# Forty weight sums moved from the first output projection to the gate and up pass

## The chip, the cores and the metric

The kernel runs on one core of a Trainium2 chip. The metric is device time in microseconds for one execution; the time of a kernel is the median of its runs. TensorE (PE in the profile) does the matrix products, VectorE (DVE) and ScalarE (ACT) work on tiles and read PE's accumulators out of PSUM, GpSimd (POOL) and SyncE (SP) mainly start DMAs. ACT can start DMAs too. Every engine executes its own list of instructions in order.

## The reference

Two layers of a backbone over 1024 latent tokens and 256 context tokens, model width 1024. Layer 0 mixes by Fourier groups and a long convolution, layer 1 by neighbourhood attention. Each mixer ends in an output projection with a gated residual, and each layer in a SwiGLU feed-forward block of width 2816:

```
h = h + g1 * (mixer(modulate(rms_norm(h))) @ w_out)
u = modulate(rms_norm(h))
h = h + g2 * ((silu(u @ w_gate) * (u @ w_up)) @ w_down)
```

In layer 0 context tokens run through the same weights as latent ones. The final RMSNorm of the latent stream is the output.

## The kernel before

Activations lie with the model dimension on partitions. Products that need float32 accuracy are made of half-precision pairs: an operand x is scaled by s, rounded to a 16-bit high part, and the rest is the low part; three products replace one. `half_split` makes a pair, the high part on ACT (line 1227) and the low part on DVE (line 1228). For s, the kernel bounds each weight block by sums of absolute values over its rows. `abs_sums` takes such a sum on ACT (line 1260, Abs with an accumulator column); a few columns are later added up over the partitions by a small matmul and inverted (`over_partitions`, `scale_cols`, `qkv_scales`, `first_scales`).

The stages around the change, in program order:

- The input projection of layer 0, with `gate_sums` woven in: the first 32 sums of layer 0's gate and up blocks, loaded by DMAs that ACT starts (`lda`, line 271) into two tiles, summed in place (line 1297).
- Convolution and Fourier stages.
- The first output projection, `out_proj`: two groups of token columns, first context and the first 512 latent tokens, then the second 512. Each group loops over eight weight blocks of 512 KB. A block is loaded by SP (`ld`), cast on ACT (line 287) with the remainder on DVE (line 289), and multiplied on PE (line 283); the accumulators are added to the residual on DVE (line 1206), squared on ACT for the coming norm (line 505) and added up (line 510). Once in each of the sixteen blocks, `next(fill, None)` advances a filler.
- That filler is `qkv_sums`: 12 sums that are left of layer 0's gate and up blocks, then 40 sums of 128x1024 tiles that layer 1 needs: 8 tiles each of the value, query, key and second output weights, and 8 of layer 1's first gate and up blocks. Each tile comes by a POOL DMA (`ldr`, line 274) into one of the 20 large tiles (`S4`). With the filler's step, the first group covers the 12 and 16 of the 40, the second group the other 24.
- The feed-forward block of layer 0, `ffn(0, ...)`. It first makes context's pass (a loop over 22 column blocks, gate and up weights split by `weights3`, with the second half of the latent operand preparation, `wino_second`, between them), and then the gate and up pass of the latent tokens: 11 rounds `i`, each with one gate and one up block of 256 columns multiplied by a seven-product scheme (`wino_steps`, line 1482; PSUM is copied by ACT at line 1487). In every round weights are fetched one step ahead, `finish` closes the round before, `sums` takes four sums of the down weights and the round's values are summed too.
- In the last round `qkv_scales` reads the sums of the 40 tiles that belong to the attention; `first_scales(1)` reads the eight of layer 1's gate and up blocks after the pass.

The order of instructions on each engine is fixed when the program is built. The program's order gives the priorities; a planner that estimates the time of every instruction places them by these and by readiness, and gives each tile a free buffer of its pool. `follow` ties instructions behind another where the program wants that. Small tiles (`S2`, 128x512 float32) have a pool of 34 buffers; `T` gives tiles from a smaller pool; `C` reserves columns for good, and `pad` fills up that area to a fixed width.

Of the kernel before, what the change touches and what calls it, by code (L numbers as in the profile page):

```python
# [14 lines left out]
AF = mybir.ActivationFunctionType  # L15
# [9 lines left out]
NFB = 22  # L25
# [4 lines left out]
WID = {0: 512, 1: 512, 2: 256, 3: 256, 4: 256}  # L30
OFF = {0: 0, 1: 512, 3: 512, 4: 768}
KSTART = (0, 8, 24, 32)
PAD_C, PAD_T, SHIFT = 136, 160, 16
BOPS = ("B11", "B21", "T2", "T1", "T3", "B22", "T4")


# [165 lines left out]
class Builder:  # L202
# [1059 lines left out]
    def qkv_sums(self):  # L1262

        a = self.a
        self.qs = self.C(40)
        src = [a["wv"][ch, kp] for ch in range(2) for kp in range(4)]
        src += [a[n][b] for n in ("wq", "wk", "w_out2") for b in range(KB)]
        src += [a[n][1, 2 * i + k] for i in (0, 1) for n in ("gate", "up") for k in (0, 1)]
        todo = [(a[("gate", "up")[j // 2 % 2]][0, j // 4 * 2 + j % 2], self.fs[:, j:j + 1])
                for j in range(32, 4 * (NFB // 2))]  # L1270
        todo += [(x, self.qs[:, k:k + 1]) for k, x in enumerate(src)]
        for j, (x, col) in enumerate(todo):
            t = self.S4()
            self.ldr(t, x)
            self.abs_sums([t], col)
            if j % 4 == 3 if j < 16 else j % 3 == 0:
                yield
        yield

    def gate_sums(self):  # L1280

        nc, a = self.nc, self.a
        n = 32
        self.fs = self.C(4 * (NFB // 2))
        tiles = {}

        def load(j):
            if j < n:
                t = tiles[j] = self.pw.tile([P, 1024], F32, tag="ws", name=self.nm("ws"))
                self.lda(t, a[("gate", "up")[j // 2 % 2]][0, j // 4 * 2 + j % 2])  # L1290

        load(0)
        load(1)
        yield
        for j in range(n):
            t = tiles.pop(j)
            nc.scalar.activation(t, t, AF.Abs, scale=2.0 ** -15, accum_out=self.fs[:, j:j + 1])
            load(j + 2)
            if j % 2:
                yield  # L1300

    def first_scales(self, l):

        keys = [(l, i, m) for i in range(2 if l else NFB // 2) for m in (0, 1)]
        n, k = len(keys), 3 * len(self.wsc)
        q = self.qs[:, 32:40] if l else self.fs
        s, inv = self.scale_cols(q, self.wcol, k, n)
        for j, key in enumerate(keys):
            self.wsc[key] = (s[:, j:j + 1], inv[:, j:j + 1])

    def qkv_scales(self):

        nc = self.nc
        bounds = self.over_partitions(self.qs[:, :32].rearrange("p (i k) -> p i k", k=1))
        t = self.C(8)
        nc.vector.tensor_reduce(t[:, :4], bounds.rearrange("p (i k) -> p i k", k=8), axis=AX, op=MAX)
        nc.vector.tensor_scalar(t[:, :4], t[:, :4], 1e-30, None, op0=MAX)
        nc.vector.reciprocal(t[:, 4:8], t[:, :4])
        self.u1col, usi = self.operand_scale(1, 0, (0, 1))
        c = self.C(3)  # L1320
        nc.vector.tensor_scalar(c[:, 2:3], t[:, 1:2], usi, 0.125, op0=MUL, op1=MUL)
        nc.vector.tensor_scalar(c[:, 0:1], c[:, 2:3], t[:, 2:3], usi, op0=MUL, op1=MUL)
        nc.vector.tensor_scalar(c[:, 1:2], t[:, 0:1], t[:, 3:4], usi, op0=MUL, op1=MUL)
        self.wscale = {n: t[:, 4 + j:5 + j] for j, n in enumerate(("wv", "wq", "wk", "w_out2"))}
        self.qinv, self.oinv = c[:, 0:1], c[:, 1:2]
# [198 lines left out]
    def ffn(self, l, u, h, hs, second, after, keep=None, begun={}):  # L1524

        nc, a = self.nc, self.a
# [6 lines left out]
        def sums(i):  # L1533

            w = a["down"][l]
            t = [self.S2() for _ in range(4)]
            a21, a22, a11, a12 = t
            with self.follow(self.last_ld):
                for x, (k, r) in zip(t, ((0, 1), (1, 1), (0, 0), (1, 0))):
                    self.ld(x, w[2 * i + k, r])  # L1540
            if i < nh:
                self.abs_sums(t, sums_of[:, 4 * i:4 * i + 4])
            nc.vector.tensor_tensor(a22, a21, a22, ADD)  # L1543
            nc.vector.tensor_tensor(a21, a11, a21, SUB)
            nc.vector.tensor_tensor(a11, a22, a11, SUB)
            nc.vector.tensor_tensor(a12, a12, a11, SUB)
            for k, x in (("S1", a22), ("S2", a11), ("S3", a21), ("S4", a12)):
                self.ldr(sops[i][k], x)

        todo = iter(())  # L1550
        if l == 0:
            self.pad(self.pt, PAD_T)
        if u is not None:
            for fb in range(NFB):
# [6 lines left out]
                t = self.T()  # L1561
# [8 lines left out]
            todo = (x for m in range(6) for x in self.ada_group(1, m, (0, 1) if m < 2 else (0,), "s4"))  # L1570

        def finish(i, gate):

            up = self.res
            inv = self.wsc[(l, i, 1)][1]
            for k, g in gate.items():
                nc.vector.scalar_tensor_tensor(g, up[k], inv, g, op0=MUL, op1=MUL)
            if i < nh:
                self.abs_sums(list(gate.values()), sums_of[:, 4 * (nh + i):4 * (nh + i) + 4])
            b11, b12, b21, b22 = gate[(0, 1)], gate[(0, 0)], gate[(1, 1)], gate[(1, 0)]  # L1580
            t1, t2, t4 = up[(0, 0)], up[(0, 1)], up[(1, 1)]
            nc.vector.tensor_tensor(t1, b12, b11, SUB)
            nc.vector.tensor_tensor(t2, b22, t1, SUB)
            nc.vector.tensor_tensor(t4, b21, t2, SUB)
            nc.vector.tensor_tensor(b12, b22, b12, SUB)
            for k, t in zip(BOPS, (b11, b21, t2, t1, b12, b22, t4)):
                self.ldr(bops[i][k], t)

        prev = None
        waiting = {}  # L1590

        def fetch(i, m):
            b = begun.get((i, m))
            if i < n2 and (b is None or not b.whole):
                g = self.weights_ahead((l, i, m), b.w) if b else self.wino_weights((l, i, m))
                next(g)
                waiting[(i, m)] = g

        fetch(0, 0)
        for i in range(n2):  # L1600
            g, up = begun.get((i, 0)), begun.get((i, 1))
            if g is None or not g.whole:
                wg = waiting.pop((i, 0))
                w = next(wg)
                next(wg)
            fetch(i, 1)
            if g is None:
                g = Steps(self.wino_steps(w, self.G))
                g.to(1)
            if prev is not None:  # L1610
                prev[0].to(7)
                finish(i - 1, prev[1])
            wu = waiting.pop((i, 1))
            w = next(wu)
            if up is None:
                up = Steps(self.wino_steps(w, self.TK))
            if i == 0:
                for k, _ in enumerate(second):
                    if k == 11:
                        next(wu)  # L1620
            next(wu, None)
            fetch(i + 1, 0)
            for k in (3, 4, 5) if i == 0 and l == 1 else ():
                g.to(k)
                up.to(k)
            g.to(5)
            up.to(1)
            if i == n2 - 1:
                scales = self.down_scales(l, nh)
                if l == 0:  # L1630
                    self.qkv_scales()
            g.to(7)
            gate = dict(self.res)
            inv = self.wsc[(l, i, 0)][1]
            for k in ((0, 0), (1, 1), (0, 1)):
                nc.scalar.activation(gate[k], gate[k], AF.Silu, scale=inv)
            t = self.G()
            nc.scalar.activation(t, gate[(1, 0)], AF.Silu, scale=inv)
            gate[(1, 0)] = t
            up.to(5)  # L1640
            prev = (up, gate)
            for k in (2 * i - 2, 2 * i - 1) if l == 1 else (9, 10) if i == 9 else (i,) if i < 9 else ():
                if 0 <= k < n2:
                    sums(k)
            for _ in range(2):
                next(todo, None)
# [903 lines left out]
```

## Time and profile before

| | us |
|---|---|
| median of 3 runs | 2923.67 |
| lowest and highest run | 2923.64, 2932.0 |
| profiled execution | 2921.78 |
| its span in the trace | 2920.0 |
| first output projection on PE | about 738 to 870 |
| context's pass on PE | about 875 to 998 |
| latent gate and up pass on PE, layer 0 | about 998 to 1389 |

The profile gives, for a stretch of the span, the busy time of each engine, the clock that PE was granted (1.00 is full speed), and the share of time in which the sixteen DMA engines were busy. A timeline row is start, duration, engine, line, operation, output and input tile; a bracket at its end gives the engine's idle time before it and what ended that.

### The profile page before, as it was taken

How to read it: one execution, taken by the hardware profiler on the slowest of the kernel's cores; microseconds unless marked ns; L12 is line 12 of the kernel's file. 1: busy time of each engine (PE TensorE's matmuls, PEld its weight loads, DVE VectorE, ACT ScalarE, POOL GpSimd, SP SyncE). 2: the span in 40 equal slices, each digit the busy share in tenths (PEclk: the TensorE clock that was granted, in tenths of full speed). 3: DMA queues.
4: the chain of work that ended last, by engine and by line, in shares of the span. 5: the costliest groups of instructions: out<-in, count | busy, mean ns of one | idle time of the engine just before them, and what ended most of it. 6: DMA issues, size and time to landing. Idle time of an engine off the chain costs nothing. (4 is left out here: it accounts for less than half of the span.)

```text
span 2920.0 us, 45967 instructions
## 1 busy us (share of the span) xinstructions
PE 2762.0 (95%) x16143; PEld 1692.6 (58%) x16143; DVE 2092.4 (72%) x3753; ACT 1653.6 (57%) x2899; POOL 644.9 (22%) x1065
## 2 busy tenths in 40 slices
PE   6979999999989999999999999999999999999998
PEld 3755546888868744444555844676665444444554
DVE  5767848586357798886886767777777688775755
ACT  4674544454666655554555554777664477654543
POOL 1011103254320121122120012454442022112000
PEclk8989999999989999999999999999999999999999
DMA  7585655357886665556995798777775666425753
GB/s 264 184 285 192 242 173 164 116 173 247 329 320 226 207 223 195 208 210 235 324 340 186 254 345 307 172 187 177 188 198 183 230 244 234 146 94 182 239 188 116
DMA packets 330915, 636.95 MB, mean 218 GB/s; under 512 B 91574, under 2 KB 131192, under 8 KB 330682
## 3 DMA queue, kind: packets, MB, share of 16 engines
q1 hardware_dynamic: 252378, 384.38, 40.6%
q0 software_dynamic: 71392, 228.65, 22.0%
q10 hardware_dynamic: 6912, 20.97, 2.1%
q8 instruction: 127, 2.08, 0.3%
q14 instruction: 106, 0.87, 0.1%
HBM read 476.30 MB, written 135.53 MB: 210 GB/s over the span
## 5 line engine op out<-in xcount | busy, mean ns | idle before, releaser
L1482 PE MATMUL ps<-s,s 128*128 128x512 f16 x2064 | 464.2, 379 | 5.3 <-ACT g L1487 3.2
L1482 PEld LDWEIGHTS <-s 128*128 128x128 f16 x2640 | 257.9, 98 | 319.1 <-issue 7.3
L283 PE MATMUL ps<-s,wh 128*128 128x256 f16 (+3 forms) x1752 | 396.4, 331 | 15.8 <-ACT wh L1227 9.9
L283 PEld LDWEIGHTS <-wh 128*128 128x128 f16 x2368 | 231.2, 99 | 194.1 <-ACT wh L1227 27.8
L1227 ACT ACTIVATE s<-s,c 128x512 f16<-128x512 f32 (+1 forms) x324 | 234.5, 752 | 137.8 <-DMA s<-d 75.3
L1699 PE MATMUL ps<-s 128*128 128x512 f16 (+2 forms) x1308 | 303.4, 378 | 2.0 <-DVE s L1228 2.0
L1228 DVE SCALAR_TENSOR_TENSOR s<-s,c,s 128x512 f16<-128x512 f32 (+1 forms) x324 | 247.4, 794 | 78.0 <-ACT s L1227 77.1
L283 PE MATMUL pq<-s,wh 128*128 128x512 f16 (+1 forms) x1000 | 281.2, 355 | 8.9 <-ACT t L1913 3.8
L283 PE MATMUL ps<-s,wl 128*128 128x256 f16 (+3 forms) x876 | 261.0, 331 | 0.5 <-DVE wl L289 0.5
L1699 PEld LDWEIGHTS <-s 128*128 128x128 f16 x1536 | 148.4, 98 | 179.0 <-issue 7.0
L274 POOL DMA_DIRECT2D d<-s x201 | 108.6, 541 | 619.2 <-DVE s L1543 200.2
L283 PE MATMUL ps<-s,s 128*128 128x65 f16 (+5 forms) x2666 | 223.0, 236 | 23.0 <-ACT s L287 5.9
L1482 PE MATMUL ps<-s,wh 128*128 128x512 f16 x616 | 186.6, 381 | 4.2 <-ACT wh L1227 4.2
L335 ACT CAST mat<-cs 128x1024 fp32r<-128x1024 f16 (+2 forms) x120 | 111.5, 935 | 134.3 <-PE ps L283 49.0
L283 PE MATMUL ps<-s,mat 128*128 128x512 f32 x696 | 181.3, 406 | 6.0 <-DVE s L289 5.4
L283 PE MATMUL pq<-s,wl 128*128 128x512 f16 (+1 forms) x500 | 174.8, 355 | 0.0
L283 PEld LDWEIGHTS <-wl 128*128 128x128 f16 x1184 | 117.6, 99 | 82.2 <-issue 6.0
L283 PEld LDWEIGHTS <-s 128*128 128x128 f16 x2400 | 114.2, 98 | 77.3 <-issue 9.7
L283 PEld LDWEIGHTS ps<-s,mat 128*128 128x128 f32 x696 | 133.9, 195 | 40.6 <-DVE s L289 6.8
L1260 ACT ACTIVATE t<-s 128x1024 bf16<-128x1024 f32 (+1 forms) x152 | 129.0, 849 | 38.3 <-DMA s<-in_down 19.6
L283 PEld LDWEIGHTS ps<-s,s 128*128 128x128 f32 (+1 forms) x746 | 114.6, 194 | 33.8 <-ACT s L287 7.1
L1482 PE MATMUL pq<-s,s 128*128 128x512 f16 x576 | 132.8, 380 | 0.3 <-ACT s L1227 0.2
(433 smaller groups left out, 5471.6 us busy)
## 6 DMA issues: line engine op xcount, KB each, us to landing
s<-d SPq DMA_DIRECT2D x294, 256.0 KB, 4.2
d<-s POOLq DMA_DIRECT2D x157, 256.0 KB, 3.8
s<-in_down SPq DMA_DIRECT2D x154, 256.0 KB, 4.9
s<-in_ada_w POOLq DMA_DIRECT2D x48, 512.0 KB, 4.9
g<-in_bias POOLq DMA_DIRECT2D x128, 192.0 KB, 3.5
s<-in_gate SPq DMA_DIRECT2D x46, 512.0 KB, 3.8
s<-in_up SPq DMA_DIRECT2D x46, 512.0 KB, 5.4
d<-g POOLq DMA_DIRECT2D x87, 256.0 KB, 2.7
```

The costliest lines, as they stand in the source:

```text
L274: self.last_ldr = self.nc.gpsimd.dma_start(out, in_).ins
L283: self.nc.tensor.matmul(o, l, r, start=st, stop=sp)
L335: self.nc.scalar.copy(m, st)
L1227: nc.scalar.activation(hi, src, AF.Copy, scale=scale)
L1228: self.last_lo = nc.vector.scalar_tensor_tensor(lo, src, scale, hi, op0=MUL, op1=SUB).ins
L1260: self.nc.scalar.activation(junk[:, :t.shape[1]], t, AF.Abs, scale=2.0 ** -15, accum_out=st[:, k:k + 1])
L1482: nc.tensor.matmul(ps, x[:, sl], y, start=first and j == 0 and x is wh and y is xh, stop=j == 3 and x is wl, skip_group_check=True)
L1699: m = nc.tensor.matmul(acc[j][:, c0:c1], x[:, sl], y[:, xs], start=first and k == 0, stop=last and k == 2, skip_group_check=True)
```

## The change

The 40 sums leave the filler of the output projection and become a filler of the gate and up pass of layer 0.

- `qkv_sums` keeps the 12 sums, two for each of the first six blocks.
- A new generator `later_sums` cuts each of the 40 tiles into two halves of 128x512. Four `S2` tiles form a ring for all 80 halves. A half is loaded by a DMA on ACT's queue (`lda`), summed in place on ACT into a column of its own, and the half four places on is loaded into the same tile.
- `ffn` of layer 0 creates the generator behind context's pass; its first step starts four loads. `some()` takes two halves at each of four places of a round, so that the 80 are used up in the first ten rounds; before `qkv_scales` whatever is left would be taken.
- There are 80 sum columns instead of 40, and the scales add two columns for each tile. `PAD_C` is smaller by 40 columns, so that the area keeps its width.

The name of the change also speaks of context's pass in half-precision pairs. That pass is already computed so in the kernel before (`weights3`), and the diff does not touch it.

```diff
-PAD_C, PAD_T, SHIFT = 136, 160, 16
+PAD_C, PAD_T, SHIFT = 96, 160, 16
...
     def qkv_sums(self):
         a = self.a
-        self.qs = self.C(40)
+        for j in range(32, 4 * (NFB // 2)):
+            t = self.S4()
+            self.ldr(t, a[("gate", "up")[j // 2 % 2]][0, j // 4 * 2 + j % 2])
+            self.abs_sums([t], self.fs[:, j:j + 1])
+            if j % 2:
+                yield
+        yield
+
+    def later_sums(self):
+        a, nc = self.a, self.nc
+        self.qs = self.C(80)
         src = [a["wv"][ch, kp] for ch in range(2) for kp in range(4)]
         src += [a[n][b] for n in ("wq", "wk", "w_out2") for b in range(KB)]
         src += [a[n][1, 2 * i + k] for i in (0, 1) for n in ("gate", "up") for k in (0, 1)]
-        todo = [(a[("gate", "up")[j // 2 % 2]][0, j // 4 * 2 + j % 2], self.fs[:, j:j + 1])
-                for j in range(32, 4 * (NFB // 2))]
-        todo += [(x, self.qs[:, k:k + 1]) for k, x in enumerate(src)]
-        for j, (x, col) in enumerate(todo):
-            t = self.S4()
-            self.ldr(t, x)
-            self.abs_sums([t], col)
-            if j % 4 == 3 if j < 16 else j % 3 == 0:
-                yield
+        src = [x[:, c:c + 512] for x in src for c in (0, 512)]
+        ring = [self.S2() for _ in range(4)]
+        for t, x in zip(ring, src):
+            self.lda(t, x)
         yield
+        for j in range(len(src)):
+            t = ring[j % 4]
+            nc.scalar.activation(t, t, AF.Abs, scale=2.0 ** -15, accum_out=self.qs[:, j:j + 1])
+            if j + 4 < len(src):
+                self.lda(t, src[j + 4])
+            yield
...
-        q = self.qs[:, 32:40] if l else self.fs
+        q = self.qs[:, 64:80] if l else self.fs
...
-        bounds = self.over_partitions(self.qs[:, :32].rearrange("p (i k) -> p i k", k=1))
+        bounds = self.over_partitions(self.qs[:, :64].rearrange("p (i k) -> p i k", k=2))
...
+        later = self.later_sums() if l == 0 else iter(())
+        next(later, None)
+
+        def some(n=2):
+            for _ in range(n):
+                next(later, None)
...
             fetch(i, 1)
+            some()
...
             fetch(i + 1, 0)
+            some()
...
             g.to(5)
             up.to(1)
+            some()
             if i == n2 - 1:
+                some(80)
                 scales = self.down_scales(l, nh)
...
             prev = (up, gate)
+            some()
```

## The prediction

> **What bounds the kernel now.** I read the page, then stretches of ten microseconds around the first output projection, the waits and timelines there, and last the stretches of the gate and up pass, which receives the work.
>
> ```profile
> span 2920.0 us, 45967 instructions
> PE 2762.0 (95%) x16143; PEld 1692.6 (58%) x16143; DVE 2092.4 (72%) x3753; ACT 1653.6 (57%) x2899; POOL 644.9 (22%) x1065
> ```
>
> TensorE (PE) is busy for 95% of the span, so a change that leaves the matmuls alone gains only where PE stands still or runs slowly. The next rows are: stretch, its length, busy time of PE, PEld, DVE, ACT and POOL (with instructions), PE's granted clock, share of the DMA engines, GB/s.
>
> ```profile
> 740.00:800.00 60.00, 60.00 (x344) 52.37 (x343) 22.70 (x34) 42.99 (x78) 17.13 (x32) 1.00 0.84 335
> 812.00:874.00 62.00, 52.19 (x201) 40.16 (x198) 35.64 (x57) 44.84 (x80) 17.04 (x32) 0.91 0.80 318
> ...
> 830.00:840.00 10.00, 8.00 (x29) 6.03 (x28) 7.40 (x10) 7.53 (x14) 5.01 (x10) 0.83 1.01 402
> 860.00:870.00 10.00, 7.60 (x24) 5.53 (x24) 1.76 (x3) 7.04 (x13) 1.63 (x3) 0.83 1.03 420
> 870.00:880.00 10.00, 6.72 (x32) 5.28 (x33) 4.13 (x5) 6.41 (x11) 0.55 (x1) 0.66 1.03 419
> 880.00:890.00 10.00, 8.06 (x52) 5.55 (x51) 5.50 (x7) 7.46 (x12) 0.54 (x1) 0.84 1.01 408
> 920.00:930.00 10.00, 10.00 (x94) 8.96 (x92) 9.12 (x12) 6.07 (x9) 1.08 (x2) 1.00 0.55 185
> ```
>
> The projection's first group (context and the first 512 tokens, 740 to 800) has busy DMA engines and ACT at 43 of 60 us, and PE does not notice: 60 of 60 at clock 1.00. The second group (812 to 874, half the work for each weight block) and the start of the context's pass lose time twice: PE idles, and its clock is lower around the idleness. By 920 all is well. PE's waits between 826 and 890 (in total, times, longest):
>
> ```profile
> PE ps L283 <- ACT wh L287: 5.9, 3, 3.5
> PE pq L283 <- DVE tk L510: 3.4, 1, 3.4
> PE ps L283 <- ACT wh L1227: 1.9, 2, 1.3
> PE ps L283 <- DVE wl L289: 0.5, 1, 0.5
> ```
>
> They lead to ACT, whose timeline (start, us, instruction, idle before it) shows what stood ahead:
>
> ```profile
> 859.65 1.04 ACT L1260 ACTIVATE t<-s 128x1024 bf16<-128x1024 f32 x1
> 860.60 0.19 ACT L1260 ACTIVATION_READ_ACCUMULATOR t<-s 128x1 f32 x1
> 860.69 1.03 ACT L287 CAST wh<-ws 128x1024 fp32r<-128x1024 f32 x1
> ...
> 870.84 1.06 ACT L1260 ACTIVATE t<-s 128x1024 bf16<-128x1024 f32 x1 [2.61 <-DMA s<-in_gate]
> 871.80 0.19 ACT L1260 ACTIVATION_READ_ACCUMULATOR t<-s 128x1 f32 x1
> 871.89 0.61 ACT L505 ACTIVATE tk<-s 128x512 f32<-128x512 f32 x1
> ```
>
> L1260 is the sum that moves. ACT works in order: the weight cast (L287) or the square (L505) that PE needs waits behind a sum, and a sum may itself wait for its load, 2.61 us here, on engines that are full (share 1.01 to 1.03 above).
>
> **What is removed.** Forty 128x1024 sums at 1.04 us of ACT, 42 us, with forty 512 KB loads issued by POOL. The sixteen whose turn comes in the first group give nothing, as PE is full there. The 24 of the second group stand behind these losses:
>
> - of the 5.9 us behind the cast, the two long waits (3.5, and 2.0 by the idle part of the stretch at 830) and the 0.5 that follows: 6.0 us. Next in line is the cast's own load and the square of the block before, so 0.4 stays;
> - of the 3.4 us before the reduction, the sum ahead of the square (870.84 to 871.89): 1.1 us. Eviction, square and addition stay;
> - 1.9 us in the context's pass, whose casts stood behind sums that waited, and whose loads shared the engines with theirs;
> - the clock: busy time times the missing share is 8.00 x 0.17 = 1.4, 7.60 x 0.17 = 1.3, 6.72 x 0.34 = 2.3 and 8.06 x 0.16 = 1.3 us. The 2.3 follow the reduction, whose idleness mostly stays; the others go: 4.0 us.
>
> Together 6.0 + 1.1 + 1.9 + 4.0 = 13.0 us. The most that these stretches could give is everything from 812 to 874 (9.8 idle, 52.19 x 0.09 = 4.7 by the clock) with 1.9 + 2.3 + 1.3 behind: 20.0 us. The least is nothing, if other work keeps the casts late.
>
> One rule speaks for less. The clock was 0.83 around the 2.0 us gap, so I let every gap cost clock. The Trainium skill, page "TensorE: Matmul & The Clock Gate", section "Why this matters for your kernels", has only PE-idle gaps above about 3 us send the clock back to half. By it the gaps of 2.0 and 1.9 us cost no clock and the sum would be 10.3; the stretch at 830 disagrees.
>
> **What is added.** Eighty 128x512 sums on ACT in a ring of four tiles, each followed by a 256 KB load on ACT's own queue. The nearest rows are half sums in the pass (start, us), ACT's loads of gate tiles earlier (min/median/max ns), and the pass's wait for the tiles of its other sums.
>
> ```profile
> 1152.85 0.63 ACT L1260 ACTIVATE t<-g 128x512 bf16<-128x512 f32 x1
> 1153.39 0.19 ACT L1260 ACTIVATION_READ_ACCUMULATOR t<-g 128x1 f32 x1
> 1153.61 0.63 ACT L1260 ACTIVATE t<-g 128x512 bf16<-128x512 f32 x1
> ...
> L271 ACTq DMA_DIRECT2D ws<-in_gate x16: 334/335/392, 177.6 to 393.8; - x16
> ...
> ACT t L1260 <- DMA s<-in_down: 16.7, 18, 2.2
> ```
>
> One half every 0.76 us and 0.33 for its load make 1.09 us, 87 in all, 8.7 in each of the ten rounds that hold eight halves; a wait, where there is one, 0.93. Behind a waiting half stand ACT's copies out of PSUM, which PE needs before it accumulates on, and the next casts. POOL is freed of forty issues in the projection; its stores there go out earlier, which nobody waits for. The four tiles come out of a pool of 34, and the 21 MB come on engines at 0.58 to 0.68. The cover is ACT's idle time in rounds of 34 us (layer 0, then layer 1's pass):
>
> ```profile
> 1001.00:1035.00 34.00, 34.00 (x159) 15.45 (x158) 34.00 (x54) 22.83 (x40) 4.31 (x8) 1.00 0.63 216
> 1035.00:1069.00 34.00, 32.54 (x152) 14.65 (x150) 33.67 (x52) 21.60 (x44) 7.15 (x14) 1.00 0.68 244
> 1069.00:1375.00 306.00, 304.31 (x1411) 137.77 (x1409) 246.69 (x392) 156.00 (x291) 69.81 (x131) 1.00 0.58 208
> sum 374.00, PE 370.85 PEld 167.87 DVE 314.37 ACT 200.43 POOL 81.28; mean PE 123.62 PEld 55.96 DVE 104.79 ACT 66.81 POOL 27.09
> ...
> 2368.00:2402.00 34.00, 34.00 (x161) 15.46 (x160) 29.34 (x53) 27.54 (x58) 8.10 (x15) 1.00 0.74 276
> 2300.00:2674.00 374.00, 368.73 (x1708) 165.81 (x1707) 279.51 (x478) 231.32 (x444) 67.86 (x126) 0.99 0.51 187
> ```
>
> A mean round has 200.43 / 11 = 18.2 us of ACT and would have 27; layer 1 has a round with 27.54 in which PE is full. Over its whole pass, with 31 us more of ACT work, PE is busy 2.1 us less. I take those 2.1 as the price, the row nearest in kind. Bounds: nothing where idle time covers it all, and 8.6 us (third rival).
>
> The sum is 13.0 - 2.1 = 10.9 us. The profiled execution took 2921.78 us (1.8 around its span) and lies 1.9 below the median; 10.9 off the median of 2923.67 gives 2912.8. About 8.8 us, 0.3%, is what a measurement of this kernel can tell from no change.
>
> **The rivals.** First: the ring does not wait for its pass. Instructions are placed by readiness, and the first row below, a store that the program has after the whole first group, was issued 59 us before that group's last eviction, the second.
>
> ```profile
> 746.31 0.55 POOL L274 DMA_DIRECT2D d<-s  x1 [1.31 <-issue]
> ...
> 805.42 1.14 DVE L1206 SCALAR_TENSOR_TENSOR s<-ps,c,s 128x256 f32<-128x256 f32 x2 [3.34 <-PE ps L283]
> ...
> ACT wh L1227 <- PE ps L283: 9.1, 10, 3.0
> ```
>
> The ring's tiles are allocated once, so only free tiles, arriving data and ACT's gaps hold it back. Drawn into the second group, halves would stand ahead of the casts as sums do now: the 3.5 and 0.5 us stay with their 1.3 of clock, 5.3 in all, and 13.0 - 5.3 - 2.1 = 5.6 us are gained: 2918.1. The change would then not do what it says.
>
> Second, on the other side: drawn into the context's pass. There a cast has the slack of the last row, 9.1 us over ten waits, 0.91. A half with its load and wait costs 1.09 + 0.93 = 2.02, so it makes a cast 1.11 us late; once in each of the 22 blocks that is 24.4 us, and 24.4 - 13.0 = 11.4 slower: 2935.1. It decides from the twelfth late block on. Against it: one late half need not stop PE, which has three pairs of weights in flight.
>
> Third: ACT becomes the bound of the pass's first rounds. With every half waiting, eight cost 8 x 2.02 = 16.2 us: 22.83 + 16.2 is 5.0 over 34, 21.60 + 16.2 is 3.8 over, and the mean of the rest, 156.00 / 9 = 17.3, stays under. About 8.6 us are paid and 4.4 gained: 2919.3. Against it: a half is loaded four places ahead, half a round.
>
> Fourth: only the long gaps cost clock, so 1.4 and 1.3 do not come back: 8.2 us, 2915.5.
>
> **How the numbers follow.** My sum gets 0.46, the ring in the second group 0.14, in the context's pass 0.18, ACT as the bound 0.12, the clock 0.10. Faster by over 8.8 us: 0.40 of the first, 0.04 of the clock, 0.02 each of the second group's and ACT's case, 0.48. Slower: 0.17, nearly all of the context case. The remaining 0.35 is within 0.3%. The range goes from 2902 (the 20.0 us, and a little for stores that also go earlier) to 2928, past the three middle cases; it leaves out some 0.04 below and 0.13 above. The likeliest case's own range is 2906 to 2918.
>
> **What would show it.** Right: PE's waits on the cast between 812 and the context's pass fall from 5.9 to about 0.4, the clock there is at 1.00 but for the reduction, the DMA share falls well below 1 and the context's pass starts about 10 us earlier; the ring's sums lie between the end of the context's pass and the tenth round, and PE loses about 5 us instead of 3.2 in the pass. Wrong: ring sums on ACT's timeline before the context's pass has ended, PE waits on L1227 in that pass, or rounds longer than 34 us.

## The result and the profile after

The changed kernel takes 2945.61 us (four runs, 2944.23 to 2949.52) beside 2924.09 for the kernel before: a ratio of 1.0069, with a 95% interval of 1.0049 to 1.0089, some 20 us slower. 2912.8 was predicted, with a range up to 2928. The profiled execution took 2946.81 us. Its page begins:

```profile
span 2945.0 us, 46018 instructions
PE 2765.8 (94%) x16143; PEld 1694.0 (58%) x16143; DVE 2093.5 (71%) x3753; ACT 1660.5 (56%) x2979; POOL 623.5 (21%) x1025
```

PE does the same work (2762.0 us before), so the time is lost where PE stands or runs slowly. Stretches of the changed kernel, with the columns of the prediction:

```profile
740.00:800.00 60.00, 60.00 (x343) 52.42 (x342) 22.23 (x34) 26.44 (x46) 8.09 (x15) 1.00 0.51 192
812.00:874.00 62.00, 56.32 (x256) 43.95 (x255) 38.64 (x57) 43.46 (x93) 4.32 (x8) 0.95 0.71 246
826.00:890.00 64.00, 54.35 (x276) 41.73 (x276) 32.78 (x43) 44.62 (x104) 4.86 (x9) 0.92 0.77 266
890.00:960.00 70.00, 49.79 (x413) 41.16 (x411) 41.09 (x52) 48.96 (x100) 4.32 (x8) 0.88 0.89 301
960.00:1020.00 60.00, 57.50 (x524) 50.74 (x521) 41.76 (x50) 41.35 (x69) 6.47 (x12) 1.00 0.78 268
```

The same stretches of the kernel before:

```profile
826.00:890.00 64.00, 52.25 (x226) 39.55 (x225) 30.55 (x39) 44.28 (x75) 17.04 (x32) 0.87 1.00 400
890.00:960.00 70.00, 70.00 (x642) 62.69 (x641) 59.73 (x74) 43.67 (x55) 7.02 (x13) 1.00 0.56 187
960.00:1020.00 60.00, 58.69 (x443) 42.97 (x442) 47.35 (x64) 38.10 (x57) 6.42 (x12) 1.00 0.60 204
```

The first group is rid of its sums (ACT 26.44 instead of 42.99 us, DMA share 0.51) and the second is a little better than before. The loss is new and lies between 890 and 960, in context's pass: 20.2 us of idle PE and 49.79 x 0.12 = 6.0 by its clock, where the kernel before lost nothing. From 826 to 1020, idle time and clock cost 42.7 us, before 19.9: 22.8 more, of the 25.0 us between the two profiled executions. PE's longest waits there (in total, times, longest):

```profile
PE ps L283 <- ACT wh L1227: 21.4, 6, 10.1
PE ps L283 <- DVE wl L1228: 4.0, 5, 0.9
PE ps L283 <- ACT wh L287: 3.6, 2, 3.2
```

1.9 us for L1227 have become 21.4. The ring's sums (line 1287: duration min/median/max in ns, first and last start):

```profile
L1287 ACT ACTIVATE s<-s x80: 612/620/637, 826.6 to 986.2; 128x512 f32<-128x512 f32 x80
```

All eighty ran in the second group and in context's pass; none is left for the pass that the code calls them from. Two things went wrong there. The first is seen on SP, which loads context's weights. SP's longest waits from 826 to 1020 (the tile names leave out end numbers: in_w_out read into an s tile is layer 1's weight, a ring load), and its timeline:

```profile
SPq L268 <- DMA s<-in_wk: 55.3, 5, 36.4
SPq L268 <- DMA s<-in_up: 32.3, 9, 7.2
SPq L268 <- DVE wl L1228: 28.6, 13, 4.1
SPq L268 <- DMA s<-in_w_out: 20.6, 6, 7.5
```

```profile
848.08 0.33 SPq L268 DMA_DIRECT2D ws<-in_w_out  x1
884.88 0.33 SPq L268 DMA_DIRECT2D s<-in_gate  x1
```

SP issued nothing for 36 us. It waited for a load of in_wk, a ring load that no weight of context needs. The program's list for SP shows why: every load that SP or ACT starts reports to one of eight semaphores, dealt out in the planned order, and the next user of a semaphore first waits for the load that had it before.

```
L268 DMA s4_2298_8784<-in_gate 128x1024 [waits DMAHW5_49,DMASW7_49]
L268 DMA s4_2301_8790<-in_up 128x1024 [waits DMAHW7_49]
```

Neither waits for a reader of its tile, both wait for another load. The load that the first one waited for, the fourth of in_wk and the 36th of the ring's 80, stood in ACT's queue:

```profile
878.69 0.63 ACT L1287 ACTIVATE s<-s 128x512 f32<-128x512 f32 x1 [1.24 <-DMA s<-in_wq]
...
879.32 1.26 ACT L534 ACTIVATE t<-c,st 128x128 f32<-128x128 f32 x4
880.60 1.28 ACT L1574 ACT_TABLE_LOAD   x1
...
881.90 0.34 ACTq L271 DMA_DIRECT2D s<-in_wk  x1
```

A ring load waits for the half that used its tile before (here 878.69), and its issue stands in ACT's order, here behind the norm's L534 and a table load. From 848.08, SP's last issue, to 881.90 ACT ran 22 halves with casts and squares between them, so SP could not fetch ahead for 36 us.

The second is seen on ACT, ahead of the cast that ended PE's longest wait (the last row is PE's):

```profile
889.06 0.63 ACT L1287 ACTIVATE s<-s 128x512 f32<-128x512 f32 x1 [1.35 <-DMA s<-in_wk]
889.07 0.82 ACTq L271 DMA_DIRECT2D s<-in_wk  x2
...
897.81 0.63 ACT L1287 ACTIVATE s<-s 128x512 f32<-128x512 f32 x1 [2.69 <-DMA s<-in_wk]
899.86 0.63 ACT L1287 ACTIVATE s<-s 128x512 f32<-128x512 f32 x1 [1.32 <-DMA s<-in_wk]
...
901.35 1.15 ACT L1227 ACTIVATE wh<-s,c 128x1024 f16<-128x1024 f32 x1 [0.15 <-issue]
...
902.55 0.61 PE L283 MATMUL ps<-s,wh 128*128 128x256 f16 x2 [10.09 <-ACT wh L1227]
```

The cast at 901.35 reads the weights that SP asked for at 884.88 (in the program's list it waits for that load's semaphore). That load took 4.0 us and had landed at 888.9, before PE stopped (892.5) and 12.5 us before the cast. So this cast did not wait for its weights: it stood in ACT's order behind halves, and halves waited for their own loads. In the second profile of the changed kernel (e5) the same cast starts 13.2 us after its weights landed, and PE waits 11.6 us. PE's second longest wait (6.3 us, until 932.77) ends with a cast at 931.57 whose weights SP had asked for at 913.62; just ahead of it three halves waited 2.5, 1.0 and 1.6 us for their loads. Wherever the trace tells when a cast's weights landed, the cast came at least 4 us later. From 885 to 960 SP's stall left weights 4 to 15 us ahead of their casts, where the kernel before had 14 to 28; but no cast waited over 0.4 us for a load of SP.

### The profile page after: what moved, and what is told of

The parts are those of the page before. It is cut to its first block, busy times and chain, and to the rows that moved or that the text cites. A ratio compares the mean times of both kernels' runs of the same rounds, so it can differ in the third digit from the quotient of the medians.

```text
span 2945.0 us, 46018 instructions
## 1 busy us (share of the span) xinstructions
PE 2765.8 (94%) x16143; PEld 1694.0 (58%) x16143; DVE 2093.5 (71%) x3753; ACT 1660.5 (56%) x2979; POOL 623.5 (21%) x1025
## 5 line engine op out<-in xcount | busy, mean ns | idle before, releaser
L1494 PEld LDWEIGHTS <-s 128*128 128x128 f16 x2640 | 257.9, 98 | 321.8 <-issue 10.9
L1227 ACT ACTIVATE s<-s,c 128x512 f16<-128x512 f32 (+1 forms) x324 | 233.2, 752 | 139.6 <-DMA s<-d 74.5
L1227 ACT ACTIVATE s<-t,c 128x512 f16<-128x512 f32 x172 | 115.1, 711 | 29.9 <-DVE t L1473 21.4
```

The source lines that it names most:

```text
L1227: nc.scalar.activation(hi, src, AF.Copy, scale=scale)
L1494: nc.tensor.matmul(ps, x[:, sl], y, start=first and j == 0 and x is wh and y is xh, stop=j == 3 and x is wl, skip_group_check=True)
```

## The experiments

Theory A: the loss comes from SP's loads of context's weights, which stand behind late ring loads on shared semaphores. Theory B: the sums occupy ACT ahead of the casts. Theory C: the ring's 21 MB fill the DMA engines. The table has every run that is compared below, each against the kernel before on its own chip (2926.6 to 2926.9 us there; its 31 runs beside the first four lie between 2912.7 and 2943.3, so medians and intervals count here, not single runs). The microseconds are the ratio's share of 2926.6. The last column is the first matmul of layer 0's down pass in the profile, which sums up all that happened until then; before it is 1388.83.

| kernel | median | ratio (95% interval) | us | down pass |
|---|---|---|---|---|
| changed, first time | 2945.61 | 1.0069 (1.0049 to 1.0089) | +20 | 1412.77 |
| e5 changed, again | 2948.84 | 1.0076 (1.0059 to 1.0092) | +22 | 1417.13 |
| e1 no sums | 2911.78 | 0.9955 (0.9941 to 0.9969) | -13 | 1379.67 |
| e3 sums, no reloads | 2929.01 | 0.9999 (0.9980 to 1.0018) | 0 | 1396.20 |
| e2 ring loaded by POOL | 2936.94 | 1.0037 (1.0021 to 1.0053) | +11 | 1395.00, e8: 1400.00 |
| e10 the same, ACT busier | 2942.45 | 1.0054 (1.0036 to 1.0072) | +16 | 1404.52 |
| e9 context's weights by POOL | 2959.02 | 1.0114 (1.0094 to 1.0134) | +33 | 1421.54 |
| e6 only the start tied | 2931.44 | 1.0026 (1.0010 to 1.0042) | +8 | 1399.82 |
| e4 paced | 2919.30 | 0.9983 (0.9965 to 1.0000) | -5 | 1384.22 |
| e7 paced, later start | 2920.30 | 0.9977 (0.9965 to 0.9990) | -7 | 1387.05 |
| e11 the same, whole sums | 2936.40 | 1.0036 (1.0022 to 1.0049) | +11 | 1399.75 |
| e12 as e7, ring loaded by POOL | 2916.72 | 0.9968 (0.9954 to 0.9983) | -9 | 1385.14 |

**e5, the changed kernel again**, on the chip of e6 to e8:

> The changed kernel itself, beside the runs that follow, on their chip. 20 us above before (2944 to 2948), as in its first measurement; the loss against the kernel without the sums is then 33 us, of which the semaphores would have some 10 (the step to POOL's loads) and the sums and bytes the rest.

It came out at 2948.84, a little above, and serves below as the second value for the changed kernel.

**e1, the sums dropped.** `later_sums` only does `nc.vector.memset(self.qs, 1.0)`.

> Leaves out the 40 moved sums and their loads altogether (the columns are set to 1.0), so its time is what the removal alone is worth. All three theories on the loss in the context's pass (late loads; ACT's occupation; full DMA engines) expect the same: 13.0 us less than before by the prediction's sum, about 2911, and 34 us less than the changed kernel; PE's waits on the cast of L287 in the second group about 0.4 us, on L1227 in the context's pass below 1 us. If it is not below 2920, the removal was mis-sized too.

Thirteen microseconds, as summed. PE from 826 to 960, and all of its waits there up to 890:

```profile
826.00:890.00 64.00, 60.97 (x384) 50.11 (x383) 45.66 (x59) 31.29 (x43) 5.94 (x11) 1.00 0.71 251
890.00:960.00 70.00, 70.00 (x644) 62.74 (x642) 58.55 (x72) 44.15 (x57) 7.03 (x13) 1.00 0.55 183
```

```profile
PE ps L283 <- ACT wh L287: 1.4, 2, 0.9
PE ps L283 <- DVE wl L1228: 0.9, 1, 0.9
PE ps L283 <- ACT wh L1227: 0.7, 1, 0.7
```

So the removal is worth its gain, and the ring where it ran costs 33 to 35 us against it.

**e3, the sums without their loads.** The four first loads stay, `lda(t, src[j + 4])` goes, and later sums take the same tiles again.

> The changed kernel with only the first four loads of the ring: the 80 sums are taken, but of those four tiles again and again, so 76 loads (20 MB) are left out. Theory A and theory C: without the loads nothing holds SP and the engines are free, PE's waits on L1227 under 3 us, 2912 to 2918. Theory B: ACT has the same 80 sums (0.76 us each, without 0.33 for the issue), the waits stay above 10 us and the time at 2930 to 2942.

```profile
L1287 ACT ACTIVATE s<-s x80: 612/617/641, 826.6 to 899.6; 128x512 f32<-128x512 f32 x80
```

```profile
PE ps L283 <- ACT wh L1227: 13.3, 3, 12.8
```

The time lies between the theories, 1 us short of B's range, and PE's waits on L1227 are B's (13.3 us, one of 12.8). The sums alone cost 13 us against e1. But with nothing to wait for they ran in one burst of 73 us, a denser one than in the changed kernel, so the 13 are B's share only roughly. And since the loads' bytes and their semaphores went together, this run does not part A from C.

**e2 and e8, the ring loaded by POOL.** `lda` becomes `ldr` in the ring; POOL's loads report to other semaphores.

> The changed kernel with the ring's 80 loads issued by POOL instead of ACT; the sums stay on ACT and as early as they are. Theory A (SP's loads of the context's weights stand behind late loads of the ring, since SP's and ACT's DMAs complete on the same eight semaphores): SP is free again, its idle time behind in_w_out and in_wk falls from 84 us in 826 to 1020 to under 20, PE's waits on L1227 in the context's pass from 21.4 to under 4 us, and the time is 2915 to 2925. Theory B (the sums occupy ACT ahead of the casts): waits stay near 21, 2938 to 2946. Theory C (engines full of the ring's 21 MB): the same as B, DMA share still 0.86 to 1.0 with PE waiting.

The profiled execution of e2 was 12 us under the median, so e8 is a second profile of the same kernel:

> The version whose ring is loaded by POOL, for a second profile, as its first one was 12 us under its median. Theory A alone (only SP's late loads hurt): PE's waits on L1227 small. A with B and C beside it (sums ahead of casts, engines near full): waits on L1227 above 9.4 us, and the clock below 0.95 in 826 to 960; SP without any wait for a load of the ring.

```profile
L1287 ACT ACTIVATE s<-s x80: 612/618/633, 830.8 to 998.8; 128x512 f32<-128x512 f32 x80
```

```profile
PE ps L283 <- ACT wh L1227: 10.9, 3, 4.9
```

```profile
876.96 0.63 ACT L1287 ACTIVATE s<-s 128x512 f32<-128x512 f32 x1 [3.04 <-DMA s<-in_wq]
...
878.71 0.63 ACT L1287 ACTIVATE s<-s 128x512 f32<-128x512 f32 x1 [1.02 <-DMA s<-in_wq]
...
879.34 1.13 ACT L1227 ACTIVATE wh<-s,c 128x1024 f16<-128x1024 f32 x1
```

The same sums at nearly the same place, the same bytes, and no wait of SP for a ring load is left among its longest. Half of PE's waits on L1227 went, and 9 to 11 us. That is less than A forecast (waits under 4 us, 2915 to 2925) and more than B and C did. What remains is in the last rows: a half that waits for its load holds the cast behind it.

Theory A is not the only reading of the gain, for in the changed kernel no cast waited over 0.4 us for its weights. The halves also wait less for their own loads: from 885 to 1000, 19.9 us in the changed kernel and 5.7 in e8, where PE's waits on L1227 are 18.6 and 6.0. ACT issues a ring load only when it comes to it: the halves at 885.31 to 886.53 were done by 887.2, but the next loads of their tiles were issued from 889.07 on, behind the half at 889.06 that waited 1.35 us for its own (rows above). From 885 on a tile's next load was issued 1.06 us after the half before it on average and 4.2 at most; in e8, by POOL, 0.41 and 0.8. Call this theory D: the ring's loads are late since their issue stands in ACT's order. The bytes are the same, so full engines alone (C) do not explain this part.

**e10 and e9, is it SP or the issue?** Taking the issues off ACT also frees ACT. e10 therefore gives ACT a small copy after each half, while POOL loads:

```diff
             nc.scalar.activation(t, t, AF.Abs, scale=2.0 ** -15, accum_out=self.qs[:, j:j + 1])
+            nc.scalar.activation(self.dummy, self.dummy, AF.Copy, scale=1.0)
```

> The ring loaded by POOL, and after each half one more small ACT instruction (a copy of 128x88, about 0.35 us) in place of the load's issue, 28 us of ACT in all. Theory A (SP's coupling was the ten microseconds between the changed kernel and the ring loaded by POOL): stays near that version, ratio 1.003 to 1.006. If the ten were ACT's time for the issues: back to the changed kernel, 1.007 to 1.008 or more. Theory B as to the rest (sums ahead of casts): some 2 to 4 us more than the version without.

```profile
PE ps L283 <- ACT wh L1227: 11.1, 4, 5.0
```

The copies took 22.0 us, 0.275 each (a group of instructions: busy time, mean ns, idle time before):

```profile
L1290 ACT ACTIVATE c<-c 128x88 f32<-128x88 f32 x80 | 22.0, 275 | 2.3
```

That is most of the 80 x 0.33 = 26 us of the issues, and it did not bring the 21.4 back: ACT's time for the issues is not what made those waits. The ratio lies half way between the two versions and its interval reaches both, so up to half of the gain may still be ACT's time. And since POOL loads here too, e10 does not part A from D. e9 leaves the ring as it is and loads context's weights by POOL (`self.ldr(st, src)` in `weights3`).

> The changed kernel with the loads of the context pass's own weights issued by POOL instead of SP; the ring stays on ACT with its loads, sums and bytes. It parts the coupling of SP to ACT (theory A) from the time that the ring's issues take on ACT. Theory A: the weights no longer stand behind the ring's loads, PE's waits on L1227 in 826 to 1020 fall from 21 to about 11 as with the ring loaded by POOL, ratio about 1.004. If ACT's issues of the ring's loads made the ten microseconds, nothing changes, ratio 1.007 to 1.008. POOL's issues wait behind its stores of the pass, which could cost some us of their own.

```profile
POOL d L274 <- DVE t L1575: 95.4, 18, 20.9
POOL d L274 <- DVE s L1206: 57.3, 8, 12.0
```

A miss: slower still. The weights now stand in POOL's queue behind stores that wait 95 us in total (18 times) and 57 us (8 times) for their data, so this run does not part A from D either, and that stays open.

**e4, the ring held to its pass.** `half_split` keeps its last ACT instruction, and every half and the four first loads follow it:

```diff
-            for _ in range(n):
-                next(later, None)
+            for _ in range(n):
+                with self.follow(self.last_act):
+                    next(later, None)
```

> The changed kernel with each half of the ring, and the four first loads, tied behind ACT's last high part of a pair (L1227) that the program had made by then, so that the ring cannot start before the context's pass ends and runs in the gate and up pass, as the prediction assumed. All theories on the context's pass: its waits vanish, that pass starts 10 us earlier than before and takes 123 us. It tells what the prediction's price of the ring in its own pass is: 2.1 us by the prediction gives 2912.8; 8.6 (ACT the bound of the first rounds) gives 2919; if A's mechanism also acts in this pass (SP's weight loads behind the ring's), more than 2925.

```profile
L1287 ACT ACTIVATE s<-s x80: 612/616/638, 991.6 to 1317.6; 128x512 f32<-128x512 f32 x80
```

That the ring ran free was the fault: same sums, same queue, same bytes, same semaphores, and 25 to 27 us less than the changed kernel. PE is busy for 60.97 us from 826 to 890 and 70.00 from 890 to 960, as in e1, and the ring lies behind context's pass. Against e1 it costs 8 us here, which is the expectation's second number, 2919.

**e6, only the start tied.** The four first loads follow context's pass, the halves are free.

> The changed kernel with only the four first loads tied behind ACT's last high part of a pair of the context's pass; the 80 halves then run freely. Asks whether the start or the pace matters. If only the place (the context's pass, whose casts have 0.9 us of slack) hurts, it equals the paced version, 2917 to 2921. If a free ring harms whatever pass it is in (80 halves in a burst of some 160 us, 0.76 + 0.33 us each plus waits, ahead of ACT's copies, and SP behind its loads), PE's waits in the gate and up pass rise from 7 to over 15 us and the time is 2928 or more.

```profile
L1287 ACT ACTIVATE s<-s x80: 612/622/635, 977.6 to 1140.6; 128x512 f32<-128x512 f32 x80
```

```profile
1000.00:1100.00 100.00, 90.89 (x403) 40.03 (x402) 79.16 (x123) 80.21 (x197) 17.28 (x32) 0.97 0.89 318
```

The free ring is spent in 163 us, as in the changed kernel (160), and costs 21 us against e1, with ACT busy for 80 of the 100 us and the DMA engines at 0.89 in the stretch shown. So a free ring hurt both passes in which it ran: tying its start is worth 13 to 15 us of the 25 to 27, and the pace the other 13.

**e7, a later start.** The first loads move from the pass's entry to the third place of round 0.

> The paced version with the first loads moved from the entry of the gate and up pass to the third of the four places of its first round. In the paced version PE entered the pass 3.8 us later than without the sums (987.64 against 983.84), waiting 4.6 us for a cast whose weights took 8.6 us to land beside the ring's four loads instead of 7.4, and were issued 2.6 us later. If the entry is where the price of the ring lies, 3 to 4 us come back: ratio 0.997, 2916 where the paced version has 2919. If the price is spread over the pass, nothing comes back.

PE did enter the pass 3.3 us earlier (984.37), but the total is the same within the intervals: the price is not the entry. The longest wait of this pass:

```profile
1058.77 3.57 PE L1494 MATMUL ps<-s,s 128*128 128x512 f16 x8 [4.07 <-ACT tk L1499]
```

```profile
1055.71 0.61 ACT L1287 ACTIVATE s<-s 128x512 f32<-128x512 f32 x1
...
1056.32 0.61 ACT L1287 ACTIVATE s<-s 128x512 f32<-128x512 f32 x1
...
1056.93 0.61 ACT L1287 ACTIVATE s<-s 128x512 f32<-128x512 f32 x1
...
1057.54 0.61 ACT L1287 ACTIVATE s<-s 128x512 f32<-128x512 f32 x1
...
1058.16 0.56 ACT L1499 COPY tk<-ps 128x512 f32<-128x512 f32 x1
```

Four halves, 2.45 us, stand in one clump ahead of the copy out of PSUM that PE waited 4.07 us for.

**e11 and e12, larger pieces, or another queue.** e11 takes 40 whole sums in a ring of two large tiles, e12 is e7 with `ldr`.

> The version with the later start, with 40 whole sums (128x1024, 1.05 us) in a ring of two large tiles instead of 80 halves: 42 us of ACT and 40 loads instead of 50 and 80. If the price in the pass (7 us against the kernel without the sums) grows with ACT's work and issues, 1 to 3 us come back: ratio 0.997. If it is the length of the piece that stands ahead of a PSUM copy (1.05 instead of 0.62 us) or a ring with only two places, it is 0.998 to 1.000.

> The version with the later start, the ring's loads issued by POOL, whose semaphores SP does not share. If SP's coupling to ACT costs something in the gate and up pass too, or ACT's issues, 2 to 4 us come back: ratio 0.9965. If the price there is the sums on ACT ahead of its PSUM copies, and the bytes, it is the same: 0.9975 to 0.998.

e11 has less ACT work and is 17 us slower than e7. PE's longest waits in its pass are on L1498, the copy out of PSUM (11.3 us in ten times); whether the 1.04 us pieces, two places or the large tiles taken from the weights do it, these runs do not part. e12 is the best that does all of the work, 9 us under the kernel before; its interval overlaps e7's, so that POOL is better than ACT there is likely and not shown.

## Why the prediction was wrong

- **What is removed: right in the sum, partly by luck.** 13.0 us were summed, e1 gives 13.2 (9.1 to 17.3); by the start of the down pass the two profiles are 9.2 apart. The parts differ, and their errors cancel in part: the wait on L287 left 1.4 instead of 0.4, the reduction's 3.4 went wholly and not by 1.1, and with it the 2.3 of clock after it; the clock of 826 to 890 went from 0.87 to 1.00, 52.25 x 0.13 = 6.8 us. Against that stands what was late next, which the sum lacked: at the entry of the gate and up pass PE waits 3.3 us in e1 for a cast, and loses 3.4 more by the clock (0.94 in 960 to 1020).
- **Where the ring lies: the step that failed.** The forecast costed the ring in the gate and up pass. The prediction saw that the tiles are allocated once and that instructions move up by readiness, and still gave 0.32 to a ring that is drawn forward. Nothing in the program ties the ring to its pass, and by the same sentence that was the case to forecast: all 80 halves ran from 826.6 to 986.2, ahead of the pass, PE's waits on L1227 rose from 1.9 to 21.4 us, and 20 to 22 us were lost where 10.9 were to be gained. Paced, the change gains 5 to 7 us, and 9 with POOL's loads: the sign that was forecast, at half the size or a little more.
- **The first rival, the second group: in part.** The ring started there, at 826.6, and L287's long wait stayed at 3.2 us (3.5 before), as it said; but the ring went on into the next pass.
- **The second rival, context's pass: the right place and sign, too small.** It said 24.4 us of loss against the removal and +11.4 in the end; the runs give 33 to 35 and +20 to +22. Its price was a late half ahead of each cast, and that is what stood ahead of the two longest waits, but in clumps: 10.1 and 6.3 us at two casts and not 1.11 at each of 22. Its counter-argument was three pairs of weights in flight. SP stood behind the ring's loads for 36 us, so when PE stopped at 892.5 only one block of the coming weights had landed, and that one waited 12.5 us for ACT. What the stall cost by itself is not shown; moving the ring's loads off ACT's queue gave 9 to 11 us (e2 against the changed kernel), which A, D and ACT's time for the issues share in parts that stay open. The "four tiles and 21 MB cost nothing" went by the DMA share of another pass, 0.58 to 0.68; where the ring ran it was 0.77 to 0.89.
- **The price of the ring in its own pass: probably mis-sized.** 2.1 us were taken, with 8.6 as the bound (its parts, 5.0 and 3.8, add up to 8.8); e4 shows 8, e7 6, e12 4, each uncertain by some 6 us, so that 2.1 was too low is likely and not shown. Layer 1's sums, the row taken, lie where there is room, and the ring lies in clumps. The price of one half was too high, though: halves in a clump follow each other in 0.61 us, the accumulator's read and the load's issue running beside, not 1.09. What costs seems to be what stands behind a clump, as in e7's longest wait, and not ACT's sum of time (third rival); no run tests that alone.
- **The clock (fourth rival): against it.** In the kernel before, a gap of 2.00 us alone was followed by five microseconds at 0.66 (the first two rows are stretches, the third is PE's timeline):

```profile
830.00:835.00 5.00, 3.00 (x14) 2.11 (x13) 5.00 (x8) 2.52 (x5) 3.43 (x7) 1.00 0.99 384
835.00:840.00 5.00, 5.00 (x17) 3.92 (x16) 2.40 (x3) 5.00 (x11) 1.58 (x3) 0.66 1.03 419
```

```profile
834.61 0.73 PE L283 MATMUL ps<-s,wh 128*128 128x512 f32 x2 [2.00 <-ACT wh L287]
```

  The 3 us below which the Trainium skill (page "TensorE: Matmul & The Clock Gate", section "Why this matters for your kernels") lets the clock stand do not hold for this gap. The gaps of 0.4 to 0.9 us in e1 left it at 1.00 from 826 to 890.

## What to carry to other kernels

Where a planner places instructions by readiness, work moved to a later place of the program is moved only if something ties it there: look for the wait that holds it, its first use of a tile or an explicit order, and pace every piece of it, since a tied start alone was 8 us slower than before and a paced ring 5 to 9 us faster. Before a queue gets loads that depend on computation, ask what shares their semaphores: a load that waits on one engine's arithmetic can hold another queue's prefetch, which no tile links to it. Before blaming a late load, look whether it had landed when its reader began: here it had, and the reader stood behind other work of its engine. And look at what stands behind a filler's clumps, not only at the engine's idle share.

## What was not expected of the hardware

- Two queues that carry different loads were not independent: SP stood for 36.4 us behind a load on ACT's queue, by the semaphores that the program deals out to both. Moving the ring's issue to POOL gained 9 to 11 us. The Trainium skill (page "DMA: Bandwidth & Descriptors", section "Issuing engines are not separate DMA queues") says that another issuing engine only saves the time of the issue on its sequencer; that alone does not account for PE's waits here: e10 put most of that time back on ACT, and they stayed at half, though its time lies half way back to the changed kernel's.
- A DMA's issue on ACT, 0.34 us, runs beside its arithmetic: the load at 881.90 was issued during an activation (L1574) that ran from 881.89 to 882.36.
